# Second-layer modulation as rows, gate matrices stored by groups of experts, prompt rows without a wait

## The chip, the cores and the metric

The kernel runs on one core of a Trainium2 chip. The metric is the device time of one execution in microseconds, as the median of several runs. All data are in f32; the heavy matmuls of the expert layers split an f32 operand into two reduced-precision parts (`uh`, `ul` and so on) and multiply three of the four pairs.

## What is computed

One step of a two-layer network on two streams of tokens: a prompt of 128 tokens and a sample of 512, width 1024. Each layer has a mixer (retention with a gated convolution in layer 0, gated DeltaNet with a convolution module in layer 1) and a layer of retrieved experts. Both are modulated by a vector for each stream:

```python
def modulation(cvec, w, b):                      # cvec: one vector for the prompt, one for the sample
    m = jax.nn.silu(cvec) @ w + b                # w: 1024 x 6144 for each layer
    return jnp.split(m[:, None, :], 6, axis=-1)

def peer_ffn(h, wq, keys, u_tab, v_tab):         # 8 heads x 16 of 16384 experts for each token
    ...
    act = jax.nn.gelu(jnp.einsum('td,tkd->tk', xt, u_tab[et]))
    return jnp.einsum('tk,tkd->td', gt * act, v_tab[et])
```

Two vectors make the modulation of a layer: a product of 2 x 1024 with 1024 x 6144.

## The kernel before

The streams are called `sp` (prompt) and `ss` (sample), each cut into tiles of 128 tokens. The order of the program is: the mixer of layer 0 for both streams; `peer_dense(ss, 0)`, the expert layer of the sample, with the prompt's work of layer 1 (`odd_p`, called as `mid`) inside it; the sample's mixer of layer 1; `peer_dense(ss, 1)`; the final norm.

The experts are computed in two ways. Three of the four sample tiles go through all 128 groups of 128 experts densely. For the fourth sample tile and for the prompt each retrieved row of the tables `u` and `v` is fetched by an indirect DMA on GpSimd (`fetch`, L1226 on) into one of six row buffers, and VectorE multiplies it: 128 rows of `u` (L1256), then 128 of `v` (L1266, into `gacc`). These are called prompt rows and sample rows here.

`peer_dense` (L1386 on) has these stages for a layer:

1. Projection (`peer_prep`). From here on a generator, `acts`, runs behind the other work: for each group of experts it loads 512 KB of `u`, splits it on ScalarE and VectorE (L1336, L1337), multiplies it with the three tiles in 24 matmuls into `A`, applies the gelu on ScalarE (L1360) and stores the result to `wd` in memory. `tick` hands it out by the time of the matmuls of the foreground, at a rate for each stage.
2. Top keys (`peer_topk`, four tiles, mostly on VectorE). In layer 0 the modulation of layer 1 is made here: at each of the 24 steps of this stage three steps of the generator `modgen` are taken (L1210). A step loads 512 KB of modulation weights on SP into a ring of three buffers (`MW`, the phase's tag `w`).
3. Gates (`gate_matrix`). For each 16 tokens of the three tiles a matrix of 128 x 128 gates for each token is built on VectorE, TensorE and ScalarE and written to memory (`gd`) as one DMA of 1 MB, 24 for a layer. The pool of this stage lies where the top keys' space and the modulation's weights lay.
4. `mid`, in layer 0 only: the prompt's mixer of layer 1 and its top keys.
5. The dense loop: for each of 128 groups of experts, `v` (512 KB), the stored activations and the gates are loaded from memory, multiplied, split, and put through 18 matmuls into `dacc`. The gates of eight groups (`GQ`) are loaded at once, in three DMAs of 512 KB. In layer 1, 53 groups are fused: their activations are computed in this loop.

In the first four stages the order of GpSimd's instructions is that of the program, and a planner with a cost model orders those of the other engines. In the dense loop the order on GpSimd, VectorE and ScalarE is that of the program.

How many gathered rows go with each group of experts in the background is set by constants: `GP` for prompt rows in the top-key and gate stages of each layer, `STEPS` for sample rows there and in `mid`, `SP` and `SF` for sample rows in the dense loop. `self.mark` is the gelu of the newest group; while it is set, and `side_rate` is zero (as it is in the stages of top keys, gates and `mid`), each gather waits for it:

```python
f = self.nc.gpsimd.indirect_dma_start(...)
if self.mark and not self.side_rate:
    self.tc.add_manual_dep(f.ins, self.mark.ins.name, ...)
```

The modulation of layer 1 is made by TensorE with the weights as the stationary operand (L350 to L354): one of 48 column groups at a time, eight products of a 128 x 128 block of weights with two columns, `c_cols[:, k, :]`, the two vectors. The result is in columns, as the mixers use it.

Of the kernel before, what the change touches and what calls it, by code (L numbers as in the profile page):

```python
# [9 lines left out]
F32 = mybir.dt.float32  # L10
# [4 lines left out]
OP = mybir.AluOpType  # L15
PSUM = bass.MemoryType.PSUM

P = 128
D = 1024
KC = 8  # L20
# [5 lines left out]
TB = 16  # L26
GQ = 8
# [3 lines left out]
NB2 = 15  # L31
NT1 = 21
RP = 0.05
GP = (1.1, 2.0)
RQ = 0.055
SQ = (0.4, 0.46)
LE = 2
# [7 lines left out]
RG = 0.12  # L45
RH = 0.27
RM = 0.7
STEPS = ({"topk": 0.0, "gates": 0.0, "mid": 2.2}, {"topk": 0.3, "gates": 0.35})
UB = 2
VB = 3  # L50
WB = 3
# [32 lines left out]
class Kern:  # L84
# [254 lines left out]
    def modulation(self, l, part):  # L339

        nc, V = self.nc, self.nc.vector
        lo, hi = PARTS[part]
        m = self.cp.tile([P, hi - lo, 2], F32, name=f"mod{l}{part}")
        on_pe = range(lo, hi) if l == 1 else range(lo + 1, hi, 2) if part == 0 else ()
        if on_pe:
            b = self.bank("mod", (P, len(on_pe), 2))
        for n in range(lo, hi):
            w = self.mw("w")
            if n in on_pe:
                nc.sync.dma_start(w, self.A[f"ada_k{l}"][on_pe.index(n) + (lo if l else 0)])  # L350
                for k in range(KC):
                    nc.tensor.matmul(b[:, on_pe.index(n), :], w[:, k * P:(k + 1) * P], self.c_cols[:, k, :],
                                     start=(k == 0), stop=(k == KC - 1))
            else:  # L354
                nc.sync.dma_start(w, self.A["ada_c"][n])
                scr = self.mw("scr")
                for s in range(2):
                    V.scalar_tensor_tensor(scr if s == 0 else w, w, 1.0, self.c_rows[s], op0=OP.mult, op1=OP.mult,
                                           accum_out=m[:, n - lo, s:s + 1])
            yield  # L360
        if on_pe:
            V.tensor_copy(m[:, on_pe.start - lo::on_pe.step, :], b)
        V.scalar_tensor_tensor(m, m, 0.5, self.ada_b[:, l, lo:hi].unsqueeze(2).to_broadcast([P, hi - lo, 2]),
                               op0=OP.mult, op1=OP.add)
        if part in (0, 2):
            g = self.gains[:, 2 * l + part // 2, :]
            V.scalar_tensor_tensor(m[:, 8:16, :], m[:, 8:16, :], 1.0, g.unsqueeze(2).to_broadcast([P, KC, 2]),
                                   op0=OP.add, op1=OP.mult)
        self.mods[l, part] = m
# [856 lines left out]
    def fetch(self, table, idx):  # L1226
        t = self.rt("row")
        f = self.nc.gpsimd.indirect_dma_start(out=t, out_offset=None, in_=table,  # L1228
                                              in_offset=bass.IndirectOffsetOnAxis(ap=idx, axis=0))
        if self.mark and not self.side_rate:  # L1230

            self.tc.add_manual_dep(f.ins, self.mark.ins.name,
                                   mybir.DependencyInfo(mybir.DependencyClass.Sync, mybir.DependencyReason.DATA))
        return t
# [56 lines left out]
    def gate_matrix(self, st, tiles, gd):  # L1291

        nc = self.nc
        V, S, PE = nc.vector, nc.scalar, nc.tensor
        for n, it in enumerate(tiles):
            cols = self.gp.tile([P, 4, P], F32, tag="gcols", bufs=1, name=self.nm("gcols"))
            for j in range(2):
                ii = self.gp.tile([P, P], I32, tag="gi", name=self.nm("gi"))
                if j == 0:
                    V.tensor_scalar(ii, st.eid[it], 7, None, op0=OP.logical_shift_right)  # L1300
                else:
                    V.tensor_scalar(ii, st.eid[it], 127, None, op0=OP.bitwise_and)
                fi = self.gp.tile([P, P], F32, tag="gf", name=self.nm("gf"))
                V.tensor_copy(fi, ii)
                b = self.bank("gT", (P, P))
                self.transpose_to(b, fi)
                V.tensor_copy(cols[:, j, :], b)
            b = self.bank("gT", (P, P))
            self.transpose_to(b, st.gate[it])
            V.tensor_copy(cols[:, 2, :], b)  # L1310
            V.tensor_scalar(cols[:, 3, :], cols[:, 0, :], -1.0, None, op0=OP.mult)
            for tb in range(P // TB):
                out = self.gp.tile([P, P, TB], F32, tag="gst", bufs=3, name=self.nm("gst"))
                for q in range(TB // 4):
                    t = tb * TB + q * 4
                    o2 = self.gp.tile([P, 4, P], F32, tag="o2", bufs=4, name=self.nm("o2"))
                    V.tensor_tensor(o2, self.iota128.unsqueeze(1).to_broadcast([P, 4, P]),
                                    cols[:, 1, t:t + 4].unsqueeze(2).to_broadcast([P, 4, P]), op=OP.is_equal)
                    b = self.bank("G", (P, 4, P))
                    for j in range(4):  # L1320
                        t = tb * TB + q * 4 + j
                        o1 = self.gp.tile([P, P], F32, tag="o1", bufs=16, name=self.nm("o1"))
                        if j == 3:

                            S.activation(o1, self.iota128, AF.Square, bias=cols[:, 3, t:t + 1])
                            S.activation(o1, o1, AF.Relu, scale=-1.0, bias=cols[:, 2, t:t + 1])
                        else:
                            V.tensor_scalar(o1, self.iota128, cols[:, 0, t:t + 1], cols[:, 2, t:t + 1],
                                            op0=OP.is_equal, op1=OP.mult)
                        self.mm(b[:, j, :], o2[:, j, :], o1, start=True, stop=True)  # L1330
                    S.copy(out[:, :, q * 4:q * 4 + 4], b.rearrange("p t i -> p i t"))
                nc.sync.dma_start(gd[n * (P // TB) + tb], out)

    def split(self, hi, lo, src):

# [50 lines left out]
    def peer_dense(self, st, l, mid=None):  # L1386

        nc, A = self.nc, self.A
        V, S, PE = nc.vector, nc.scalar, nc.tensor
        tiles, gt = list(range(st.nt - 1)), st.nt - 1  # L1390
        N = len(tiles) * P
        NTB = N // TB
        gd = self.tc.dram_tile([NTB, P, P, TB], F32, name=self.nm("gd"))
        wd = self.tc.dram_tile([P, P, N], F32, name=self.nm("wd"))
        n = FUSED[l]
        LA = (LA0, LA1)[l]
        fused = {e for e in range(4, P) if e * n // P != (e + 1) * n // P}
        gg, got = {}, {}
# [4 lines left out]
        def load(e):  # L1403

            if e >= P:
                return
            vr = ld("vr", [P, D], bufs=LA + 1)
            nc.sync.dma_start(vr, A[f"v{l}"][e * P:(e + 1) * P, :])
            for n in range(0, NTB, 8):
                if e == 0 or e % GQ == 4 + n // 8 and e + GQ < P:  # L1410
                    g = e // GQ + (e > 0)
                    if n == 0:
                        gg[g] = ld("gt", [P, NTB, GQ, TB], bufs=2)
                    nc.sync.dma_start(gg[g][:, n:n + 8],
                                      gd[n:n + 8, :, g * GQ:(g + 1) * GQ, :].rearrange("b p i t -> p b i t"))
            if e in fused:
                w = self.u_load(l, e, up, UB)
            else:
                w = ld("w", [P, N], bufs=LA + 1)
                nc.sync.dma_start(w, wd[e])  # L1420
            got[e] = [vr, w, gg[e // GQ]]
# [6 lines left out]
        with self.banks(5), self.tc.tile_pool(name=self.nm("up"), bufs=2, reuse_waits="tile") as up:  # L1428
# [13 lines left out]
            self.rate, self.side_rate = RA, 0.0  # L1442
            self.steps_per_act, self.side_per_act = STEPS[l]["topk"], GP[l]
            with self.topk_space():
# [28 lines left out]
        with ExitStack() as c2:  # L1473
# [33 lines left out]
            for e in range(P):  # L1507
# [12 lines left out]
                for n in range(len(tiles)):  # L1520
                    ts = slice(n * P, (n + 1) * P)
                    for i, wh, wl, vh, vl in ends:
                        for lhs, rhs, fi, la in ((wh, vh, True, False), (wh, vl, False, False), (wl, vh, False, True)):
                            for half in range(2):
                                self.mm(accs[n][half], lhs[:, ts], rhs[:, half * 512:(half + 1) * 512],
                                        start=(i == 0 and fi), stop=(i == P - 1 and la))
# [5 lines left out]
            g = self.bcast_cols(self.mod(l, 3)[:, :, st.s:st.s + 1], "ga2", [gr[:, 0:512], gr[:, 512:1024]], self.bankA)  # L1532
# [149 lines left out]
def _chunks(w):  # L1682

    n = w.shape[1] // P
    return np.ascontiguousarray(w.reshape(KC, P, n, P).transpose(2, 1, 0, 3)).reshape(n, P, KC * P)


def _halves(w):

    return np.ascontiguousarray(w.reshape(4, 2, P, 512).transpose(0, 2, 1, 3)).reshape(4, P, 1024)  # L1690


def _cols(v):

    return np.ascontiguousarray(v.reshape(-1, P).T)


def device_inputs(inp):
    a = {k: np.asarray(v) for k, v in inp.items()}
    d = dict(_constants())  # L1700
    d["x_p"], d["x_s"] = a["x_prompt"][0], a["x_sample"][0]
    d["cT"] = np.ascontiguousarray(np.stack([_cols(a["c_ctx"]), _cols(a["c"][0])], axis=2))
    d["ada_k0"], d["ada_k1"] = _chunks(a["ada_w"][0])[1:16:2], _chunks(a["ada_w"][1])
    d["c_rows"] = np.stack([a["c_ctx"], a["c"][0]])
    d["ada_c"] = np.ascontiguousarray(a["ada_w"][0].T).reshape(48, P, D)
    d["ada_b"] = np.ascontiguousarray(np.stack([_cols(a["ada_b"][l]) for l in range(2)], axis=1))
# [12 lines left out]
    w = a["ev_w_in"][0]  # L1719
    t = _chunks(w)  # L1720
    q, bg, cg, hb = t[0:4], t[12:16], t[16:20], t[20:24]
# [3 lines left out]
    w = a["od_w_in"][0]  # L1725
# [40 lines left out]
```

## Time and profile before

| | us |
|---|---|
| median of three runs (lowest, highest) | 4222.24 (4215.71, 4222.56) |
| profiled execution, its own time | 4210.32 |
| its span, first to last instruction | 4208.6 |
| TensorE busy | 3844.7 (91%) |
| VectorE busy | 3396.4 (81%) |
| ScalarE busy | 1501.1 (36%) |
| GpSimd busy | 1455.3 (35%) |

The rows below come from one profiled execution; times are counted from the start of its span. "PE" is TensorE, "PEld" its weight loads, "DVE" VectorE, "ACT" ScalarE, "POOL" GpSimd and "SP" the engine that issues most DMAs. A clock of 1.00 is 2.4 GHz, 0.50 is 1.2 GHz. Most matmuls and many helpers go through one line (L162), so the tile's name says what an instruction belongs to: `A` is an expert's activation, `dacc` the dense accumulation, `mod` the modulation, `gacc` the gathered rows' sum. An f32 matmul appears as two instructions.

### The profile page before, as it was taken

How to read it: one execution, taken by the hardware profiler on the slowest of the kernel's cores; microseconds unless marked ns; L12 is line 12 of the kernel's file. 1: busy time of each engine (PE TensorE's matmuls, PEld its weight loads, DVE VectorE, ACT ScalarE, POOL GpSimd, SP SyncE). 2: the span in 40 equal slices, each digit the busy share in tenths (PEclk: the TensorE clock that was granted, in tenths of full speed). 3: DMA queues.
4: the chain of work that ended last, by engine and by line, in shares of the span. 5: the costliest groups of instructions: out<-in, count | busy, mean ns of one | idle time of the engine just before them, and what ended most of it. 6: DMA issues, size and time to landing. Idle time of an engine off the chain costs nothing. (4 is left out here: it accounts for less than half of the span.)

```text
span 4208.6 us, 57302 instructions
## 1 busy us (share of the span) xinstructions
PE 3844.7 (91%) x19934; PEld 3246.7 (77%) x19934; DVE 3396.4 (81%) x7163; ACT 1501.1 (36%) x2796; POOL 1455.3 (35%) x1080
## 2 busy tenths in 40 slices
PE   6788879999999998899998989789989989999997
PEld 4453559999998897688885458759989968888886
DVE  6568799993898975988887999669887877778888
ACT  2110133221565443333332254533335733333333
POOL 0106563111233342344434765033010024444443
PEclk9999589877999999999999999999999999999998
DMA  8539698657899988999997977158355789999996
GB/s 293 180 132 365 217 349 289 239 210 248 279 330 349 339 290 287 319 365 357 352 319 300 336 246 258 55 173 296 110 188 196 259 311 325 326 330 329 343 339 217
DMA packets 439634, 1162.04 MB, mean 276 GB/s; under 512 B 39728, under 2 KB 190640, under 8 KB 432944
## 3 DMA queue, kind: packets, MB, share of 16 engines
q1 hardware_dynamic: 284656, 595.23, 40.5%
q0 software_dynamic: 154688, 563.15, 37.7%
q8 instruction: 156, 2.56, 0.2%
q14 instruction: 134, 1.10, 0.1%
HBM read 1062.48 MB, written 95.75 MB: 275 GB/s over the span
## 5 line engine op out<-in xcount | busy, mean ns | idle before, releaser
L1228 POOL DMA_INDIRECT row<-v,eid x512 | 740.8, 1447 | 1331.3 <-DVE gacc L1266 607.2
L162 PE MATMUL A<-hHL,uh 128*128 128x384 f32 x4096 | 1101.7, 349 | 20.1 <-ACT uh L1336 19.2
L1228 POOL DMA_INDIRECT row<-u,eid x512 | 684.9, 1338 | 1153.3 <-ACT w L1360 483.3
L162 PEld LDWEIGHTS A<-hHL,uh 128*128 128x128 f32 x4096 | 768.9, 196 | 32.4 <-ACT uh L1336 23.6
L162 PE MATMUL A<-hHL,ul 128*128 128x384 f32 x2048 | 714.1, 350 | 44.3 <-DVE ul L1337 44.1
L1266 DVE SCALAR_TENSOR_TENSOR gacc<-row,gel,gacc 128x1024 f32<-128x1024 f32 x508 | 650.4, 1280 | 100.2 <-DMA row<-v,eid 95.6
L1256 DVE SCALAR_TENSOR_TENSOR row<-row,hn 128x1024 f32<-128x1024 f32 x512 | 614.2, 1218 | 114.1 <-DMA row<-u,eid 112.6
L162 PE MATMUL dacc<-vh,wh 128*128 128x512 f32 x1536 | 483.5, 396 | 51.3 <-ACT wh L1336 51.3
L162 PE MATMUL pt<-hT,w 128*128 128x128 f32 (+1 forms) x2176 | 456.5, 367 | 27.7 <-DMA w<-wq 15.6
L162 PE MATMUL dacc<-vl,wh 128*128 128x512 f32 x1536 | 477.6, 392 | 0.0
L1336 ACT CAST uh<-ur 128x1024 fp32r<-128x1024 f32 x256 | 268.3, 1048 | 563.8 <-PE A L162 441.8
L162 PEld LDWEIGHTS A<-hHL,ul 128*128 128x128 f32 x2048 | 400.5, 196 | 53.5 <-DVE ul L1337 52.1
L162 PEld LDWEIGHTS pt<-hT,w 128*128 128x128 f32 x2176 | 306.0, 197 | 171.4 <-issue 145.8
L162 PE MATMUL dacc<-vh,wl 128*128 128x512 f32 x1536 | 391.4, 389 | 0.0
L162 PEld LDWEIGHTS dacc<-vh,wh 128*128 128x128 f32 x1536 | 283.2, 189 | 124.7 <-ACT wh L1336 73.6
L1336 ACT CAST wh<-w 128x384 fp32r<-128x384 f32 (+1 forms) x235 | 137.5, 585 | 660.5 <-DVE w L1498 471.6
L1337 DVE TENSOR_TENSOR ul<-ur,uh 128x1024 fp32r<-128x1024 f32 x256 | 311.8, 1218 | 75.5 <-ACT uh L1336 75.0
L1337 DVE TENSOR_TENSOR vl<-vr,vh 128x1024 fp32r<-128x1024 f32 x256 | 312.8, 1222 | 65.6 <-ACT vh L1336 63.4
L162 PEld LDWEIGHTS dacc<-vl,wh 128*128 128x128 f32 x1536 | 290.9, 189 | 62.7
L162 PEld LDWEIGHTS dacc<-vh,wl 128*128 128x128 f32 x1536 | 288.6, 188 | 60.1
L1336 ACT CAST vh<-vr 128x1024 fp32r<-128x1024 f32 x256 | 267.7, 1046 | 57.3 <-PE dacc L162 48.7
L1337 DVE TENSOR_TENSOR wl<-w,wh 128x384 fp32r<-128x384 f32 (+1 forms) x235 | 152.2, 648 | 126.4 <-ACT wh L1336 126.3
(365 smaller groups left out, 5096.0 us busy)
## 6 DMA issues: line engine op xcount, KB each, us to landing
ur<-ut SPq DMA_DIRECT2D x256, 512.0 KB, 4.9
vr<-v SPq DMA_DIRECT2D x256, 512.0 KB, 6.8
gd<-gst SPq DMA_DIRECT2D x48, 1024.0 KB, 5.2
gt<-gd SPq DMA_DIRECT2D x96, 512.0 KB, 8.8
wd<-w SPq DMA_DIRECT2D x203, 192.0 KB, 3.4
w<-wd SPq DMA_DIRECT2D x203, 192.0 KB, 6.9
w<-ada_k SPq DMA_DIRECT2D x56, 512.0 KB, 6.0
w<-wq SPq DMA_DIRECT2D x48, 512.0 KB, 5.2
```

What stands on the lines that cost most here:

```text
L162: self.nc.tensor.matmul(out, lhsT, rhs, start=start, stop=stop)
L1228: f = self.nc.gpsimd.indirect_dma_start(out=t, out_offset=None, in_=table, in_offset=bass.IndirectOffsetOnAxis(ap=idx, axis=0))
L1256: V.scalar_tensor_tensor(u, u, 1.0, hn, op0=OP.mult, op1=OP.mult, accum_out=act[:, k:k + 1])
L1266: V.scalar_tensor_tensor(gacc, v, t[:, k:k + 1], gacc, op0=OP.mult, op1=OP.add)
L1336: self.nc.scalar.copy(hi, src)
L1337: self.nc.vector.tensor_tensor(lo, src, hi.bitcast(F32), op=OP.subtract)
```

## The change

The modulation of layer 1 turns its operands round. The two vectors are the stationary operand (128 x 2) and the weights move, 512 columns at a time: for each of twelve groups of 512 outputs, eight products, two for each weight load of 512 KB. The result is two rows of 512, which ScalarE copies from PSUM into a buffer of the weights' ring; four small transposes on TensorE bring it back into columns, and VectorE copies these. The modulation of layer 0 stays as it was. The number of generator steps (48) and of loads (48 of 512 KB) stays too.

The gate matrices are stored as `[group of 8, 128, blocks of tokens, 8, 16]` instead of `[block of tokens, 128, 128, 16]`: a write of 1 MB now goes to 16 places for each partition, 512 B each, and a load of 512 KB reads 4 KB in one piece for each partition, where it read eight pieces of 512 B.

Gathers wait for the newest expert's gelu if they belong to the sample (an empty `lane`) and no longer by the stage; prompt rows (`lane` "p") never wait for it. And three constants go up: 1.5 prompt rows for each group of experts in layer 0 (1.1 before), and 0.45 and 0.6 sample rows in the top-key and gate stages of layer 1 (0.3 and 0.35 before).

```diff
-GP = (1.1, 2.0)
+GP = (1.5, 2.0)
-STEPS = ({"topk": 0.0, "gates": 0.0, "mid": 2.2}, {"topk": 0.3, "gates": 0.35})
+STEPS = ({"topk": 0.0, "gates": 0.0, "mid": 2.2}, {"topk": 0.45, "gates": 0.6})
...
+            for o in range(lo // 4, hi // 4):
+                b = self.bank("mod")
+                for kp in range(KC // 2):
+                    w = self.mw("w")
+                    nc.sync.dma_start(w, self.A["ada_m1"][o, kp])
+                    for k in (2 * kp, 2 * kp + 1):
+                        nc.tensor.matmul(b[0:2, :], self.c_cols[:, k, :], w[:, (k % 2) * 512:(k % 2 + 1) * 512],
+                                         start=(k == 0), stop=(k == KC - 1))
+                    yield
+                t = self.mw("modr")[0:2, 0:512]
+                nc.scalar.copy(t, b[0:2, :])
+                b = self.bank("modT", (P, 4, 2))
+                for j in range(4):
+                    nc.tensor.transpose(b[:, j, :], t[:, j * P:(j + 1) * P], self.ident[0:2, 0:2])
+                V.tensor_copy(m[:, 4 * o - lo:4 * o - lo + 4, :], b)
...
-        if self.mark and not self.side_rate:
+        if self.mark and not self.lane:
...
-                nc.sync.dma_start(gd[n * (P // TB) + tb], out)
+                nc.sync.dma_start(gd[:, :, n * (P // TB) + tb].rearrange("g p q t -> p g q t"),
+                                  out.rearrange("p (g q) t -> p g q t", q=GQ))
...
-        gd = self.tc.dram_tile([NTB, P, P, TB], F32, name=self.nm("gd"))
+        gd = self.tc.dram_tile([P // GQ, P, NTB, GQ, TB], F32, name=self.nm("gd"))
...
-                    nc.sync.dma_start(gg[g][:, n:n + 8],
-                                      gd[n:n + 8, :, g * GQ:(g + 1) * GQ, :].rearrange("b p i t -> p b i t"))
+                    nc.sync.dma_start(gg[g][:, n:n + 8], gd[g, :, n:n + 8])
```

## Rows read from the trace of the kernel before

**Rows 1.** The page's first part: busy time of each engine, share, instructions.
```profile
PE 3844.7 (91%) x19934; PEld 3246.7 (77%) x19934; DVE 3396.4 (81%) x7163; ACT 1501.1 (36%) x2796; POOL 1455.3 (35%) x1080
```
**Rows 2.** Windows: stretch, length, busy PE, PEld, DVE, ACT, POOL; clock, DMA share, GB/s.
```profile
800.00:1060.00 260.00, 256.59 (x1438) 255.27 (x1437) 170.18 (x491) 51.48 (x69) 44.94 (x31) 0.78 0.66 233
1060.00:1340.00 280.00, 262.16 (x1739) 256.86 (x1738) 261.97 (x554) 172.89 (x376) 90.91 (x68) 0.99 0.89 318
```
**Rows 3.** The modulation's own busy time in that window; then timeline, start and length.
```profile
800.00:1060.00 260.00, 110.93 (x768) 112.31 (x768) 2.71 (x14) 0.00 (x0) 0.78 0.66 233
...
1042.92 7.05 PE L352 MATMUL mod<-c_cols,w 128*128 128x2 f32 x48
...
1050.31 0.22 DVE L1300 TENSOR_SCALAR gi<-eid 128x128 int32<-128x128 int32 x1
```
**Rows 4.** Timeline of the stretch: two modulation blocks that follow each other.
```profile
964.36 7.00 PE L352 MATMUL mod<-c_cols,w 128*128 128x2 f32 x48
...
981.25 6.84 PE L352 MATMUL mod<-c_cols,w 128*128 128x2 f32 x48
```
**Rows 5.** Windows of one microsecond around the first of these blocks.
```profile
966.00:967.00 1.00, 1.00 (x11) 1.00 (x10) 0.15 (x1) 0.00 (x0) 0.92 (x1) 1.00 1.00 397
967.00:968.00 1.00, 1.00 (x10) 1.00 (x11) 1.00 (x1) 0.00 (x0) 0.69 (x2) 0.95 1.02 376
...
970.00:971.00 1.00, 1.00 (x6) 1.00 (x6) 0.00 (x0) 0.00 (x0) 0.00 (x0) 0.50 1.11 283
...
976.00:977.00 1.00, 1.00 (x8) 1.00 (x7) 0.00 (x0) 0.00 (x0) 0.00 (x0) 1.00 0.47 193
```
**Rows 6.** Timeline: f32 matmuls, transposes; chain of waits: one expert's matmuls.
```profile
2439.78 5.74 PE L162 MATMUL pn<-w,hT 128*128 128x512 f32 x13
...
210.99 1.04 PE L416 MATMUL xT<-cst,xn 128*128 128x128 f32 x8
...
4153.44 4.16 PE A L162 x24
```
**Rows 7.** A window in the sample's retention, and the timeline at its end.
```profile
440.00:450.00 10.00, 10.00 (x33) 7.81 (x34) 8.31 (x15) 2.58 (x10) 7.66 (x5) 0.50 0.82 263
...
447.76 5.49 PE L162 MATMUL s<-qk,qk 64*128 64x512 f32 x6
```
**Rows 8.** Windows of line L1266 (v rows), VectorE; list of waits: total, times, longest.
```profile
800.00:1060.00 260.00, 37.48 (x30) 0.78 0.66 233
1060.00:1210.00 150.00, 34.55 (x27) 1.00 0.86 301
...
POOL row L1228 <- ACT w L1360: 753.8, 94, 139.7
```
**Rows 9.** DMA issues by line: count, KB each, median us to landing.
```profile
vr<-v SPq DMA_DIRECT2D x256, 512.0 KB, 6.8
gd<-gst SPq DMA_DIRECT2D x48, 1024.0 KB, 5.2
gt<-gd SPq DMA_DIRECT2D x96, 512.0 KB, 8.8
...
w<-ada_k SPq DMA_DIRECT2D x56, 512.0 KB, 6.0
```
**Rows 10.** Windows of the two dense loops, layer 0 and layer 1.
```profile
1690.00:2205.00 515.00, 499.77 (x2184) 410.32 (x2185) 443.35 (x606) 190.66 (x251) 210.60 (x118) 0.99 0.99 346
3420.00:4183.00 763.00, 739.52 (x3510) 636.22 (x3508) 614.58 (x773) 256.45 (x356) 335.51 (x229) 1.00 0.93 324
```
**Rows 11.** Windows, layer 1 before its loop: all engines, then L1256 (u rows, two records each).
```profile
3000.00:3400.00 400.00, 350.29 (x2189) 340.65 (x2189) 334.95 (x1006) 207.15 (x421) 32.80 (x21) 0.96 0.60 205
...
3000.00:3420.00 420.00, 25.47 (x42) 0.95 0.62 213
```
**Rows 12.** Timeline of the end: the dense tiles' last additions, and the gathered tile.
```profile
4186.95 1.87 DVE L1289 TENSOR_TENSOR x_s<-x_s,dacc 128x512 f32<-128x512 f32 x3
...
4194.01 1.29 DVE L1288 TENSOR_TENSOR gacc<-gacc,vr 128x512 f32<-128x512 f32 x2
```

More of the change, by code (lines that the diff above doesn't have):

```diff
@@ L343, in modulation @@
         m = self.cp.tile([P, hi - lo, 2], F32, name=f"mod{l}{part}")
[L344 to L360, printed above, removed]
@@ L361, in modulation @@
-        if on_pe:
-            V.tensor_copy(m[:, on_pe.start - lo::on_pe.step, :], b)
+        if l == 0:
+            on_pe = range(lo + 1, hi, 2) if part == 0 else ()
+            if on_pe:
+                b = self.bank("mod", (P, len(on_pe), 2))
+            for n in range(lo, hi):
+                w = self.mw("w")
+                if n in on_pe:
+                    nc.sync.dma_start(w, self.A["ada_k0"][on_pe.index(n)])
+                    for k in range(KC):
+                        nc.tensor.matmul(b[:, on_pe.index(n), :], w[:, k * P:(k + 1) * P], self.c_cols[:, k, :],
+                                         start=(k == 0), stop=(k == KC - 1))
+                else:
+                    nc.sync.dma_start(w, self.A["ada_c"][n])
+                    scr = self.mw("scr")
+                    for s in range(2):
+                        V.scalar_tensor_tensor(scr if s == 0 else w, w, 1.0, self.c_rows[s], op0=OP.mult, op1=OP.mult,
+                                               accum_out=m[:, n - lo, s:s + 1])
+                yield
+            if on_pe:
+                V.tensor_copy(m[:, on_pe.start - lo::on_pe.step, :], b)
+        else:
+            for o in range(lo // 4, hi // 4):
+                b = self.bank("mod")
+                for kp in range(KC // 2):
+                    w = self.mw("w")
+                    nc.sync.dma_start(w, self.A["ada_m1"][o, kp])
+                    for k in (2 * kp, 2 * kp + 1):
+                        nc.tensor.matmul(b[0:2, :], self.c_cols[:, k, :], w[:, (k % 2) * 512:(k % 2 + 1) * 512],
+                                         start=(k == 0), stop=(k == KC - 1))
+                    yield
+                t = self.mw("modr")[0:2, 0:512]
[4 more added lines that the diff above has]
+                V.tensor_copy(m[:, 4 * o - lo:4 * o - lo + 4, :], b)
@@ L1702, in device_inputs @@
     d["cT"] = np.ascontiguousarray(np.stack([_cols(a["c_ctx"]), _cols(a["c"][0])], axis=2))
-    d["ada_k0"], d["ada_k1"] = _chunks(a["ada_w"][0])[1:16:2], _chunks(a["ada_w"][1])
+    d["ada_k0"] = _chunks(a["ada_w"][0])[1:16:2]
+    d["ada_m1"] = np.stack([_halves(a["ada_w"][1][:, o:o + 512]) for o in range(0, 6 * D, 512)])
     d["c_rows"] = np.stack([a["c_ctx"], a["c"][0]])
```

## The prediction, made before the result was known

> **What bounds the kernel now.** I read the busy times first [rows 1]: TensorE is busy for 91% of the span and VectorE for 81%, so a saving must come from a stretch where TensorE has no gaps, and VectorE must have room for what is pushed together. Then the windows by stage [rows 2]. The stretch from 800 to 1060 us, in which the first expert layer picks its top keys and the second layer's modulation is made, stands out: TensorE is busy for 256.6 of 260 us, but its mean granted clock is 0.78, while the stretch behind it has 0.99. VectorE is busy for only 170 us there. The expert-weighting stage (gate matrix) cannot begin before the last modulation matmul, because its pool takes over the memory of the modulation's weights: the last block of 48 modulation matmuls starts at 1042.9 us and lasts some 7 us, and the first gate instruction starts at 1050.31 [rows 3]. So TensorE's time in this stretch is on the path.
>
> The timeline inside the stretch is periodic [rows 4]: a block of 48 modulation instructions (three weight tiles, 16 each) begins at 964.36 and the next at 981.25, a period of 16.9 us. The stretch has 768 such instructions [rows 3], 16 periods. The block takes 7.0 us, the two experts' matmuls behind it 9.9. In windows of one microsecond [rows 5] the clock is full at 966, begins to fall at the end of 967, is half at 970 (in the block) and full again at 976, well into the experts' matmuls. The modulation now loads 128x128 weights to stream two columns, and the chip takes the clock down to 1.2 GHz under it.
>
> **The modulation as rows.** Removed: 384 products of two columns, 768 instructions. Added: 96 products with two stationary columns and 512 moving ones, two instructions each as for any f32 matmul here, 192 in all, 12 for three weight tiles. Thirteen f32 matmuls of 512 columns take 5.74 us at full clock [rows 6]; less the 0.59 us of the last, that is 0.429 us from start to start. Twelve take 5.15 us. Two experts are 48 instructions; 24 take 4.16 us at full clock [rows 6], so 8.3 us. Per period there are three of the 48 small transposes (eight take 1.04 us [rows 6], less one's 0.27: 0.11 each) and a little wait, 0.4 us. The new period is 8.3 + 5.15 + 0.4 = 13.9 us instead of 16.9 if the clock stays full: 3.0 us x 16 = 48 us. Note where it comes from: at full clock the old block would need about as long as the new one (its instructions come twice as densely before 968 as after). The gain is the clock, 1.8 us in the block and 1.6 in the experts behind it, less the transposes.
>
> Added beside it: 12 ScalarE copies and 12 instead of 4 small VectorE copies; ScalarE is busy for 51 of 260 us [rows 2], so they are covered. The transposes wait for the copy, and the next expert's matmuls stand behind them on TensorE: nothing if the planner puts an expert in between, up to 12 x 1.5 us = 18 us if not (ScalarE's instructions there average 51.48 / 69 = 0.75 us [rows 2]; the copy and one ahead of it); I take the 6 us that stand in the period. The copied row takes one of the three weight buffers, so 60 allocations pass where 48 did; a weight load lands in 6.0 us [rows 9] and the experts behind a block last 8.3, so it still fits, with 2 us left. The loads stay 48 of 512 KB on SP.
>
> Does it reach the end? VectorE must do its 170 us in 212. Prompt rows freed from their wait add to that (below): 27 of them are now done after 1060 at 1.28 us [rows 8], 35 us; if all move ahead, 205 of 212 us are full. So I take 40 of the 48.
>
> **Prompt rows without the wait.** In the top-key and gate stages each prompt gather now waits for the newest expert's activation: 754 us of GpSimd waiting are put down to it [rows 8], and 30 v rows go through in 260 us although VectorE has room for more. After it they flow as buffers come free, and 1.5 instead of 1.1 go with each expert. The work is the same; 27 rows leave the gate stage of 1060 to 1340, where VectorE is busy for 262 of 280 us. Bound: -35 us if that stage is VectorE's alone, +10 us if rows stand ahead of the splits that TensorE waits for; TensorE is busy for 262 there too, so I take -5.
>
> **Gate matrices by groups.** Each of 48 writes of 1 MB goes from runs of 8 KB to runs of 512 B, each of 96 reads from 512 B to 4 KB. Price of short runs: the 512 KB gate read lands in 8.8 us, the 512 KB load of v issued just ahead of it in 6.8 [rows 9]. Of the 2.0 us 1.5 is its own transfer at 346 GB/s [rows 10], so 0.5 us per 512 KB is left, 1 us for a write: 24 us of queue in a 280 us stage whose DMA share is 0.89, to 0.97. Ends: 0 and, with the whole 2.0 us, 96 us of queue, which would fill that stage; I take the near one, 0 us on the path, SP and the three gate buffers absorbing it. The dense stages lose 24 us of queue each at a share of 0.99 and 0.93, but TensorE is busy there for 500 of 515 and 740 of 763 us [rows 10]: -4 us, ends 0 and -20. The Trainium skill (Perfetto Trace Analysis, DMA Optimizations) says transfers under 2 KB carry a significant overhead each; by that the writes would cost more than I allow. The reads of 512 B here show at most 0.5 us per 512 KB; no run yet shows such writes.
>
> **More sample rows early in layer 1.** 21 u rows (42 records) are now done before the dense loop [rows 11]; that loop steps 53 x 2.3 + 75 x 1.5 = 234 rows, so some are left over and end the kernel: VectorE adds the last dense tile by 4188.82 but starts scaling the gathered rows at 4194.01 [rows 12]. Rates of 0.45 and 0.6 for 0.3 and 0.35 bring some 10 rows forward: the leftover is gone, -5 us (0 to -8). They cost 10 x 1.3 = 13 us of VectorE in 3000 to 3400, where it is busy for 335 of 400 [rows 11]: 0 to 13, I take +3.
>
> **Sum.** -40 - 5 + 0 - 4 - 5 + 3 = -51 us. The profiled execution took 4210.3 us (span 4208.6), 11.9 below the median of the runs, 4222.2. From 4210.3 to 4159; on the median, 4171.
>
> **The rivals.** They hang on one question the trace cannot settle: whether two stationary columns keep the clock up. Against it: from 440 to 450 TensorE is busy without a gap, on a mix of 64-row and 128-row matmuls, and has half clock all along [rows 7]; a busy engine is not enough, part of the array in use may count. For it: those lack rows, while the new matmuls use all 128 rows and stream without gaps. The Trainium skill (TensorE: Matmul & The Clock Gate, Why this matters for your kernels) says to keep TensorE busy continuously to get full clock; by that my forecast holds, but [rows 7] disagree with it as it stands.
>
> Rival 1, the clock falls as now: nine matmuls in the 3.9 us before it falls, three at 0.86, 6.4 us, plus 0.5 and the 9.9 us of experts: 16.8, no gain. The rest gives -11: 4211. On the median between 4203 and 4228.
>
> Rival 2, slower: the clock stays low through every block, as it does at 440. Twelve at 0.86 us are 10.3, plus 0.6 and 9.9: 20.8, +3.9 x 16 = +62, less 11: 4273, 4235 to 4290. It decides if a block starts at 0.50.
>
> Rival 3, VectorE takes over: the clock holds, but the freed rows and the top keys fill VectorE, and the gate stage waits for it. The gain is halved to 20: 4191.
>
> Rival 4, more gain: the gate stage is VectorE's and gives back 35 us: about 4140.
>
> **How the numbers follow.** Forecast 0.52 (4150 to 4190), rival 1 0.23, rival 2 0.12, rival 3 0.08, rival 4 0.05. About 0.2% (8 us) can be told from no change here. Faster: forecast, rivals 3 and 4 and a third of rival 1, 0.72. Same: most of the rest of rival 1, 0.14. Slower: rival 2 and a little of rival 1, 0.14. The range goes from rival 4's end to the end of rival 1: 4135 to 4230; rival 2 and a little at the other end are left out.
>
> **What would show it.** Right: a granted clock near 1.0 from 800 on, modulation matmuls of 512 columns 0.43 us apart, the first gate instruction near 1010 and the layer's dense loop some 45 us earlier. Wrong: windows of 0.5 in the blocks (rivals 1, 2); a full clock but VectorE without gaps up to the gate stage (rival 3). For the rows: POOL's waits for the expert's activation well under 754 us, prompt rows done by about 1060. For the layout: gate reads nearer to 6.8 us, and gate writes not far above their 5.2 us [rows 9]. For the tail: gathered rows scaled right after the last dense tile.

## The result, and the profile after

| | before | after |
|---|---|---|
| median of the runs, us (lowest, highest) | 4218.98 (4213.36, 4222.56) | 4158.94 (4148.63, 4168.12) |
| ratio after to before, 95% interval | | 0.9858 (0.9831 to 0.9885) |
| profiled execution, its own time | 4210.32 | 4148.63 |
| its span | 4208.6 | 4146.9 |

The change takes off 60 us (49 to 71). The prediction said 4171, 4135 to 4230, faster. In the profiled executions the span is 61.7 us shorter, and the page's first part says where: TensorE is busy for 3808.5 us instead of 3844.7 [rows 1], 36.2 less, so the other 25.5 us are gaps on TensorE that closed.

```profile
PE 3808.5 (92%) x19406; PEld 3124.2 (75%) x19406; DVE 3393.6 (82%) x7171; ACT 1510.3 (36%) x2810; POOL 1457.4 (35%) x1080
```

The windows of after (stretch, length, busy PE, PEld, DVE, ACT, POOL with their instructions, clock, DMA share, GB/s) answer to [rows 2], [rows 10] and the tail:

```profile
800.00:1060.00 260.00, 255.58 (x1110) 167.74 (x1108) 208.43 (x532) 70.23 (x95) 77.05 (x47) 0.99 0.81 294
1060.00:1340.00 280.00, 267.36 (x1852) 262.83 (x1852) 255.12 (x647) 175.32 (x388) 67.61 (x50) 0.99 0.89 297
...
1652.00:2156.00 504.00, 497.26 (x2172) 408.15 (x2173) 433.17 (x553) 187.07 (x247) 210.45 (x118) 1.00 0.95 347
3330.30:4146.00 815.70, 759.71 (x3592) 653.49 (x3592) 643.01 (x818) 273.19 (x389) 333.29 (x226) 0.97 0.87 315
```

In the stretch of the modulation the granted clock went from 0.78 to 0.99. TensorE is as busy as before (255.6 and 256.6 us), and what changed is what it did: 192 of its 1110 instructions are the modulation and 48 the small transposes, which leaves 870, 36 experts of 24, where before 768 of 1438 left 670, 28 experts. The stretch did eight experts more, 8 x 4.16 = 33 us of TensorE at full clock [rows 6].

The modulation's own busy time in that window, and the timeline of TensorE around the place of [rows 4]:

```profile
800.00:1060.00 260.00, 88.99 (x192) 12.79 (x192) 0.99 0.81 294
...
960.89 5.31 PE L372 MATMUL mod<-w,c_cols 128*2 128x512 f32 x12
969.28 1.88 PE L372 MATMUL mod<-w,c_cols 128*2 128x512 f32 x4
975.28 0.40 PE L379 MATMUL modT<-cst,modr 2*128 2x2 f32 x4
```

The block of twelve takes 5.31 us where the one of 48 took 7.0 [rows 4]; the stretch's total is 88.99 us instead of 110.93 [rows 3].

The last matmul of the modulation did not come earlier. The first row below is its group (duration in ns: lowest, median, highest; then first and last start), the second the first gate instruction, which stands behind it at 1064.83 and stood at 1050.31 [rows 3].

```profile
L372 PE MATMUL mod<-w,c_cols x192: 591/592/593, 815.0 to 1059.6; 128*2 128x512 f32 x192
...
1064.83 0.22 DVE L1318 TENSOR_SCALAR gi<-eid 128x128 int32<-128x128 int32 x1
```

The gate stage is what got shorter. From its first copy of a gate matrix to its last it took 259.1 us before (1071.2 to 1330.3) and 193.9 after (1079.7 to 1273.6). Prompt rows are out of it; the windows of their `v` rows (the line that was L1266 [rows 8]):

```profile
800.00:1060.00 260.00, 67.13 (x53) 0.99 0.81 294
1060.00:1210.00 150.00, 0.00 (x0) 0.99 0.78 247
```

All 53 lie in the first stretch, where 30 and 27 lay in the two. The dense loop of layer 0 begins at 1652.6 instead of 1698.8, 46 us earlier, and takes 503.4 us in both. The last gate copy of layer 1 is at 3330.3 instead of 3385.3, 55 us earlier, and the span ends 62 us earlier.

### The profile page after: what moved, and what is told of

It reads as the page before. It is cut to its first block, busy times and chain, and to the rows that moved or that the text cites. A ratio compares the mean times of both kernels' runs of the same rounds, so it can differ in the third digit from the quotient of the medians.

```text
span 4146.9 us, 56434 instructions
## 1 busy us (share of the span) xinstructions
PE 3808.5 (92%) x19406; PEld 3124.2 (75%) x19406; DVE 3393.6 (82%) x7171; ACT 1510.3 (36%) x2810; POOL 1457.4 (35%) x1080
## 5 line engine op out<-in xcount | busy, mean ns | idle before, releaser
L1246 POOL DMA_INDIRECT row<-v,eid x512 | 751.1, 1467 | 1084.4 <-DVE gacc L1284 629.8
L162 PE MATMUL A<-hHL,uh 128*128 128x384 f32 x4096 | 1085.0, 344 | 14.6 <-ACT uh L1355 11.3
L162 PEld LDWEIGHTS A<-hHL,uh 128*128 128x128 f32 x4096 | 748.6, 191 | 46.6 <-issue 20.3
L162 PE MATMUL A<-hHL,ul 128*128 128x384 f32 x2048 | 705.3, 345 | 44.7 <-DVE ul L1356 44.6
L162 PEld LDWEIGHTS A<-hHL,ul 128*128 128x128 f32 x2048 | 391.4, 191 | 67.5 <-DVE ul L1356 51.0
```

What stands on the lines that cost most here:

```text
L162: self.nc.tensor.matmul(out, lhsT, rhs, start=start, stop=stop)
```

## The experiments

Two questions: which part of the change gives how much, and why. The ratios are to the kernel before, run on the same chip between the others; the microseconds are the ratio's distance from 1 times 4217.

| | modulation | prompt rows | layout | sample rates | ratio (95%) | us |
|---|---|---|---|---|---|---|
| e1 | new | old | old | old | 0.9902 (0.9878 to 0.9927) | -41 |
| e2 | old | new | old | old | 0.9962 (0.9945 to 0.9980) | -16 |
| e5 | old | old | new | old | 1.0045 (1.0028 to 1.0063) | +19 |
| e6 | old | old | old | new | 0.9963 (0.9946 to 0.9979) | -16 |
| e10 | old | new | new | old | 0.9966 (0.9951 to 0.9981) | -14 |
| e3 | old | new | new | new | 0.9913 (0.9890 to 0.9936) | -37 |
| e9 | new | old | new | new | 0.9933 (0.9911 to 0.9954) | -28 |
| e7 | new | new | old | new | 0.9865 (0.9847 to 0.9882) | -57 |
| e8 | new | new | new | old | 0.9864 (0.9845 to 0.9884) | -57 |
| after | new | new | new | new | 0.9858 (0.9831 to 0.9885) | -60 |

**The modulation alone, put into the kernel before.**

```diff
-                    nc.tensor.matmul(b[:, on_pe.index(n), :], w[:, k * P:(k + 1) * P], self.c_cols[:, k, :],
+                        nc.tensor.matmul(b[0:2, :], self.c_cols[:, k, :], w[:, (k % 2) * 512:(k % 2 + 1) * 512],
```

> The kernel before with the modulation as rows alone. Theory C (clock): the gain is TensorE's clock under the modulation; the experts that it does more of by 1060 us are missing from the gate stage. Then this alone gives most of the gain, 35 to 48 us of the 60, and the granted clock of 800 to 1060 is near 1.0. Theory V (VectorE): the gate stage became shorter because the prompt rows left it. Then this gives 10 us at most, and the gate stage stays near 285 us.

The weights are stored in another order for this, still 4 KB in one piece for each partition and load. Measured: 4178.44 (4174.98 to 4188.68), 41 us less than before (31 to 51). The window from 800 to 1060 has a granted clock of 0.99 and VectorE is busy for 191.6 us of it. TensorE is busy for 3817.1 us in the whole, 27.6 less than before. So the modulation gives most of the 60 us under the old rule for the rows too. Its profiled execution (4180.92) is 29.4 us under before's: the gate stage takes 234.5 us instead of 259.1, the dense loop of layer 0 begins 17 us earlier, and another 12 us are gained later, between the first addition of a dense tile in layer 0 and the last gate copy of layer 1 (1142.1 us instead of 1154.0), where nothing of the new modulation runs. That last part is not explained.

**The prompt rows alone.**

```diff
-GP = (1.1, 2.0)
+GP = (1.5, 2.0)
-        if self.mark and not self.side_rate:
+        if self.mark and not self.lane:
```

> The kernel before with the prompt rows' part alone (no wait for the experts, 1.5 instead of 1.1 with each in layer 0). Theory C: between -10 and +5 us, as TensorE's work in 800 to 1060 stays at a clock of 0.78. Theory V: -25 to -40 us, with the gate stage near 240 us.

Measured: 4206.77 (4188.73 to 4211.94), 16 us less (8 to 23). The gate stage ends 32 us earlier, at 1298.7, but the dense loop of layer 0 begins only 9 us earlier, at 1689.4: the experts that the shorter gate stage no longer covers are done in `mid`. From the end of the gate stage to the dense loop TensorE has 2282 instructions (2173 before); the 109 more are 4.5 experts, 19 us at 4.16 [rows 6]. This profiled execution is the slowest of e2's ten (4211.94) and ends 1.6 us after before's, with 10 us more in layer 1; so the trace shows what happens in the two stages, and not where the 16 us of the medians come out.

**The old modulation in the changed kernel.**

```diff
-                    for k in (2 * kp, 2 * kp + 1):
-                        nc.tensor.matmul(b[0:2, :], self.c_cols[:, k, :], w[:, (k % 2) * 512:(k % 2 + 1) * 512],
+                    nc.tensor.matmul(b[:, on_pe.index(n), :], w[:, k * P:(k + 1) * P], self.c_cols[:, k, :],
```

> The changed kernel with the old modulation back. Theory C: 40 to 55 us slower than the changed kernel (4200 to 4215 us), clock back to about 0.78 in 800 to 1060. Theory V: at most 10 us slower.

Measured: 4182.73 (4177.66 to 4188.70), 24 us slower than the changed kernel (8 to 38 by the two ratios), for the 41 of e1 (31 to 51); these overlap. TensorE is busy for 3835.4 us, 26.9 more than in the changed kernel. So on TensorE's own time the new modulation is worth 27 us in both places; what reaches the end is 24 to 41 by the two medians. And the three other parts together give 37 us here, where the prediction had 11. That opened the question that the next runs are about.

**Half of the rows of the array.** The products of the modulation run over 64 of the 128 rows, so half of each sum is left out.

```diff
-nc.tensor.matmul(b[0:2, :], self.c_cols[:, k, :], w[:, (k % 2) * 512:(k % 2 + 1) * 512],
+nc.tensor.matmul(b[0:2, :], self.c_cols[0:64, k, :], w[0:64, (k % 2) * 512:(k % 2 + 1) * 512],
```

> The changed kernel with the modulation's products over 64 of the 128 rows, so that half of each sum is left out; as many instructions of the same length. If the chip counts the rows of the array that are in use, as the 64-row matmuls near 440 us suggest, the clock falls to 0.5 in the modulation blocks and the kernel loses 30 to 60 us. If it counts matmuls in flight only, the clock stays at 1.0 and the time within 10 us of the changed kernel's.

Measured, one execution: 4187.50 us, granted clock 0.96 from 800 to 1060. This windows view of three microseconds each is of e4:

```profile
959.00:962.00 3.00, 3.00 (x13) 1.35 (x11) 3.00 (x4) 0.00 (x0) 0.00 (x0) 1.00 0.64 242
962.00:965.00 3.00, 1.79 (x9) 1.31 (x9) 3.00 (x4) 1.42 (x2) 0.00 (x0) 1.00 0.10 35
965.00:968.00 3.00, 3.00 (x7) 0.53 (x7) 3.00 (x4) 0.03 (x1) 0.00 (x0) 0.74 0.91 276
968.00:971.00 3.00, 3.00 (x10) 3.00 (x11) 3.00 (x4) 0.55 (x1) 0.00 (x0) 0.50 0.91 289
971.00:974.00 3.00, 3.00 (x13) 3.00 (x12) 0.26 (x1) 0.00 (x0) 0.00 (x0) 0.62 0.41 165
974.00:977.00 3.00, 3.00 (x20) 2.74 (x19) 2.20 (x3) 1.44 (x2) 0.00 (x0) 1.00 0.37 96
```

The blocks between 902 and 962 keep the full clock with half of the rows. Where it falls next, that is behind a gap: TensorE is busy for 1.79 of the 3 us from 962 (it waits 1.21 us for a split), and then the clock is 0.74 and 0.50 with no gap left. The changed kernel does the same behind the one long gap of its stretch from 800 to 1060, 2.04 us at 837 to 839:

```profile
836.00:839.00 3.00, 1.09 (x8) 0.62 (x6) 3.00 (x5) 2.71 (x3) 1.54 (x2) 1.00 1.03 420
839.00:842.00 3.00, 2.87 (x12) 2.87 (x13) 3.00 (x7) 0.00 (x1) 2.27 (x2) 0.72 1.02 406
842.00:845.00 3.00, 3.00 (x14) 2.81 (x12) 3.00 (x5) 0.14 (x1) 0.49 (x1) 0.71 1.04 420
845.00:848.00 3.00, 3.00 (x8) 0.59 (x8) 3.00 (x5) 1.40 (x2) 2.35 (x1) 1.00 1.03 388
```

Not every gap is followed by a fall. In e4 one of 2.85 us, longer than either, ends at 845.2, and the clock is full on both sides of it:

```profile
841.00:845.00 4.00, 1.36 (x9) 0.78 (x7) 4.00 (x6) 2.71 (x3) 2.37 (x2) 1.00 1.03 412
845.00:849.00 4.00, 3.79 (x22) 3.79 (x23) 4.00 (x8) 0.00 (x0) 0.94 (x1) 1.00 1.03 414
```

So half of the rows did not take the clock down, in blocks of 1.9 to 3.6 us with experts on the whole array between them; a longer run of such matmuls was not tried. The old blocks have another shape, two moving columns for each 128x128 of weights, and no gap in the record [rows 5]. What in them took the clock down was not taken apart; shown is that turning the operands round ended it. The time of this one execution, some 28 us above the changed kernel's median, fits neither expectation (30 to 60, or within 10) and is not settled: it has 24 us of gaps on TensorE from 800 to the end of its gate stage, the changed kernel 13.

**The layout alone, and the sample rates alone.**

```diff
-        gd = self.tc.dram_tile([NTB, P, P, TB], F32, name=self.nm("gd"))
+        gd = self.tc.dram_tile([P // GQ, P, NTB, GQ, TB], F32, name=self.nm("gd"))
```

> The kernel before with the gate layout alone. The old modulation with freed prompt rows, the new layout and the new sample rates came out 37 us below before, the freed prompt rows alone 13: some 24 us belong to the layout, to the sample rates, or to neither alone. Theory L (layout): reads in one piece for each partition end stalls of the dense loops and the gate stage: 15 to 20 us less, near 4202, the dense loops shorter. Theory S (sample rows) and theory N (where the planner puts the experts once rows move, no part by itself): within 5 us of before, 4215 to 4224, both dense loops within 3 us of 504 and 799 us.

```diff
-STEPS = ({"topk": 0.0, "gates": 0.0, "mid": 2.2}, {"topk": 0.3, "gates": 0.35})
+STEPS = ({"topk": 0.0, "gates": 0.0, "mid": 2.2}, {"topk": 0.45, "gates": 0.6})
```

> The kernel before with 0.45 and 0.6 sample rows in the top-key and gate stages of layer 1 alone. Theory S: the gathered rows no longer end the kernel and fill gaps of VectorE in layer 1: 15 to 20 us less, near 4202. Theory L and theory N: 2 us less (the tail -5, the extra VectorE time +3, as predicted), between 4207 and 4225; the last gathered row is added before the last dense tile in any case.

Measured: the layout alone is slower, 4238.17 (4222.56 to 4242.74), 19 us (12 to 27), which no theory had. The rates alone give 4201.65 (4191.93 to 4212.51), 16 us less (9 to 23), as theory S had it.

**Each of these two taken back in the changed kernel** (the same diffs, read backwards).

> The changed kernel with the gate matrices stored by blocks of tokens as before. Theory L: 15 to 20 us slower than the changed kernel, near 4176. Theory S and N: within 6 us of it, 4155 to 4165; its gate writes are issued in 320 ns again instead of 370.

> The changed kernel with the old rates of sample rows in layer 1 (0.3 and 0.35). Theory S: 15 to 20 us slower than the changed kernel, near 4176, with gathered rows scaled some 5 us after the last dense tile again. Theory L and N: 2 us slower (0 to 8), 4159 to 4167.

Measured: 4159.74 (4157.49 to 4162.84) and 4160.68 (4155.33 to 4164.81). Neither can be told from the changed kernel, so theory L is out, and theory S with it as an account of the changed kernel. For the layout there are two numbers, +19 alone (12 to 27) and -3 here (-17 to 11 by the two ratios), whose intervals do not overlap, if only just. A new theory was needed: the parts meet in the gate stage.

**The theory of the meeting parts.** Two more kernels complete the square of prompt rows and layout. The first is the changed kernel with the two lines of e2's diff taken back, the second is before with e2's and the layout's diffs.

> The changed kernel with the old rule for the prompt rows (each gather waits for the newest expert's activation in these stages) and 1.1 of them with each group of experts. The layout alone made the kernel before 22 us slower, and taking it out of the changed kernel made no difference. Theory I (the parts meet: gate writes in short pieces cost time only while the gathers of prompt rows share the DMA queues of the gate stage): here both come together again, so this is slower than the changed kernel by the 13 us of the rows and the 22 us of the layout, near 4194 (4185 to 4200), with a gate stage at a DMA share of 0.9 or more and late loads of u. Theory A (each part has its own price, the 22 us are an accident of the order): 13 us slower, 4168 to 4177.

> The kernel before with the freed prompt rows (and 1.5 of them) and the gate layout, the other parts as before. Theory I: the rows have left the gate stage, so its writes have room: as the rows alone, 4200 to 4212. Theory A: the rows' 13 us off and the layout's 22 on, near 4226 (4220 to 4234).

Measured: 4186.81 (4181.21 to 4193.78), where theory I had 4185 to 4200 and theory A 4168 to 4177; and 4198.62 (4188.95 to 4212.63), where theory I had 4200 to 4212 and theory A 4220 to 4234. Both are theory I's, the second 1.4 us below its range. The prompt rows are worth 16 us with the old layout, and with the new one 33 (e5 to e10) and 32 (e9 to after). The layout costs 19 us while prompt rows are in the gate stage and, once they are out, +2 (e2 to e10) and -3 (e7 to after).

The profile shows how. Windows of the gate stage, first gate copy to last, one kernel each: before; the layout alone; rows and layout; old rows in the changed kernel; the old layout in it. After's own has the values 193.90 us, DMA share 0.90.

```profile
1071.20:1330.30 259.10, 243.20 (x1630) 238.89 (x1630) 245.53 (x520) 160.56 (x356) 84.70 (x62) 0.99 0.88 316
```
```profile
1078.80:1357.30 278.50, 251.41 (x1648) 247.33 (x1647) 246.89 (x520) 160.12 (x357) 81.12 (x63) 0.96 0.91 297
```
```profile
1066.00:1294.10 228.10, 220.51 (x1513) 217.10 (x1511) 191.19 (x454) 153.20 (x345) 38.24 (x29) 0.99 0.84 269
```
```profile
1081.20:1326.00 244.80, 217.89 (x1457) 212.79 (x1457) 227.56 (x504) 150.36 (x342) 79.90 (x57) 0.95 0.92 300
```
```profile
1087.70:1280.50 192.80, 184.56 (x1304) 182.00 (x1303) 184.03 (x453) 140.38 (x327) 38.32 (x31) 0.98 0.79 290
```

With the rows in the stage (GpSimd busy for some 80 us) the layout takes the DMA share from 0.88 to 0.91 while the rate falls from 316 to 297 GB/s: the queues work longer for the same bytes, and the stage gets longer. With the rows out (38 us) there is room: from 0.79 to 0.90 in the changed kernel, 0.90 x 193.9 - 0.79 x 192.8 = 22 us of queue for 24 writes (the other pairs that differ in the layout give 18 to 25), and the stage is as long as it was. The mean share does not tell after (0.90) from e5 (0.91). The first half of the stage does, where almost no rows are left in after; first e5, then after:

```profile
1078.80:1218.00 139.20, 135.89 (x919) 135.03 (x919) 125.55 (x250) 85.79 (x190) 36.28 (x27) 1.00 0.91 290
1079.70:1176.70 97.00, 97.00 (x723) 97.00 (x722) 91.46 (x241) 79.26 (x192) 1.33 (x2) 1.00 0.78 232
```

What the busy queues delay is read from the waits of that stage (waiter, awaited, us, times, longest): the loads of `u`, then the splits, then TensorE. Before, then e5, then after:

```profile
ACT uh L1336 <- DMA ur<-ut: 25.7, 9, 4.4
...
PEld A L162 <- ACT uh L1336: 14.5, 9, 3.9
```
```profile
ACT uh L1337 <- DMA ur<-ut: 49.6, 14, 6.0
...
PEld A L162 <- ACT uh L1337: 25.7, 10, 7.8
```
```profile
ACT uh L1355 <- DMA ur<-ut: 4.1, 3, 1.7
...
PEld A L162 <- ACT uh L1355: 0.9, 1, 0.9
```

ScalarE waits for late `u` 25.7 us before, 49.6 with the layout alone, 4.1 after. TensorE's weight loads wait 14.5, 25.7 and 0.9 us for the split behind it. The same wait in the stage in e1 and e9 (rows in, old and new layout; e9's sample rates act in layer 1 only), then in e2, e10 and e7 (rows out: old, new, old):

```profile
ACT uh L1354 <- DMA ur<-ut: 4.5, 2, 2.6
ACT uh L1355 <- DMA ur<-ut: 28.4, 7, 6.5
...
ACT uh L1336 <- DMA ur<-ut: 0.5, 1, 0.5
ACT uh L1337 <- DMA ur<-ut: 0.9, 2, 0.6
ACT uh L1354 <- DMA ur<-ut: 3.3, 3, 1.4
```

With the rows in, the layout adds 24 us of late `u` beside either modulation (25.7 to 49.6, 4.5 to 28.4); with the rows out it adds less than 1 (0.5 to 0.9, 3.3 to 4.1). This is what theory I says, and e9 had the share (0.92) and the late loads that it named. The rows alone do not make `u` late: e1 has them in the stage and waits 4.5 us. Not all of e5's distance is the stage's. Its profiled execution, the slowest of its six, is 32 us over before's: 8 are lost ahead of the stage, 19 in it and 5 in layer 1 ahead of its gates' end.

**How far this goes.** Two kernels on either side of the new constants:

```diff
-GP = (1.5, 2.0)
+GP = (1.35, 2.0)
```

> The changed kernel with 1.35 instead of 1.5 prompt rows for each group of experts, the smallest disturbance of the order that we could find: it measures what a mere reordering is worth. Theory I: the rows still end ahead of the gate stage, so nothing: 4152 to 4168. If prompt rows reach into the gate stage again, 5 to 15 us slower.

```diff
-GP = (1.5, 2.0)
-STEPS = ({"topk": 0.0, "gates": 0.0, "mid": 2.2}, {"topk": 0.45, "gates": 0.6})
+GP = (2.0, 2.0)
+STEPS = ({"topk": 0.0, "gates": 0.0, "mid": 2.2}, {"topk": 0.6, "gates": 0.9})
```

> The changed kernel with still more gathered rows early: 2.0 prompt rows for each group of experts, 0.6 and 0.9 sample rows in layer 1. Theory I: the prompt rows already end ahead of the gate stage, so nothing is left to win there: 4150 to 4170. A theory in which VectorE has room left in layer 1 gives up to 10 us less, 4145 to 4155.

Measured: 4156.64 (4142.23 to 4162.16), ratio to before 0.9865 (0.9839 to 0.9891), the same as the changed kernel; and 4169.59 (4164.69 to 4176.39), 0.9894 (0.9868 to 0.9921), some 11 to 15 us slower than the changed kernel by the medians and the ratios, though the intervals overlap. A little fewer rows change nothing, since they still end ahead of the gate stage; many more do not help. In e12 TensorE is busy for 250.6 us from 800 to 1060, five less than in the changed kernel, at a clock of 0.97: gaps opened there again. No kernel tried is better than the changed one by what can be measured.

## Why the prediction was right, point by point

**What bounds the kernel.** Right. The clock of the stretch from 800 to 1060 was the largest thing to win, and e1 alone has 41 of the 60 us.

**The modulation as rows.** The cause was right, and rivals 1 and 2 are out: the clock does not fall in the blocks. The size was not quite: the forecast was 3.0 us for each of 16 periods, 48, of which 40 reach the end. The stretch gained 33 us of experts, TensorE's busy time 27 (e1, and e3 against after), the runs 41 and 24. Of the terms, the block of twelve was put at 5.15 us and took 5.31 where it stands whole; over the stretch it is 88.99 / 16 = 5.56, because the planner cuts most blocks into fours (1.88 us each), and the experts cost (255.6 - 89.0 - 4.8) / 36 = 4.5 us, not the 4.16 of the fastest row. The 4.8 is 12 times the transposes' 0.40; that and the copy were put at 0.4 us a period, which held: ScalarE's copy takes 576 ns and one wait of 0.4 us is put down to it.

The place was wrong. The gate stage was to begin near 1010, and it began at 1065, later than before. The planner did not pull the modulation forward; it put eight more experts into the same stretch, and the saving arrived where these experts were missing, as a shorter gate stage. The dense loop of layer 0 then did begin 46 us earlier, for the 45 forecast.

The Trainium skill (TensorE: Matmul & The Clock Gate, Why this matters for your kernels) asks for a TensorE that is kept busy. The new blocks agree (clock 1.00 in 5.31 us without a gap); the old blocks do not, busy for 1.00 of 1.00 us at a clock of 0.50 [rows 5]. The doubt drawn from [rows 7], that rows in use may count, was answered by e4 for blocks of up to 3.6 us: 64 of 128 rows kept the full clock. What holds it at 0.50 from 440 to 450 stays open; TensorE is busy for only 31 of the 50 us from 400 on, and the two falls shown above follow gaps too.

**Prompt rows.** The step that was mis-sized. Forecast -5, bounds -35 to +10; measured -16 alone and some -32 with the new layout. The lower bound's reason (VectorE's time leaves the gate stage) was there: VectorE is busy for 191 us of it in e10, for 247 in e5. What the step did not see is the DMA side: the gathers of these rows left the stage too, and with them the late loads of `u` (25.7 us before, 0.5 in e2; 49.6 in e5, 0.9 in e10). The argument "TensorE is busy there too, so -5" took TensorE's gaps there, 18 us of that window [rows 2], for small. With the new layout it is these gaps that close: 27.1 us in the stage of e5 and 7.6 in e10's (278.5 - 251.4 and 228.1 - 220.5), 26.9 in e9's and 8.2 in after's, 19 of the 33 and 32 us. The stage's clock rises as well, from 0.96 to 0.99 and from 0.95 to 0.98; what that is worth was not measured by itself. With the old layout the clock there is 0.99 with the rows and without, 6 of 16 us of gaps close (e2), and where the rest of the -16 comes from stays open.

**Gate matrices by groups.** The price in queue was right and the cover was not named. Put at 1 us of queue for a write, measured 22 / 24 = 0.9 (0.7 to 1.1 over the pairs); put at 0.5 us for a read, measured (1.00 - 0.95) x 504 / 48 = 0.5 us, from the DMA share of layer 0's loop, 0.95 above and 1.00 in before's window of it:

```profile
1698.00:2202.00 504.00, 496.77 (x2171) 407.86 (x2172) 433.58 (x552) 187.61 (x246) 210.60 (x118) 1.00 1.00 348
```

The reading that the read's price came from does not hold, though. It took the 2.0 us by which a gate read lands after the load of `v` [rows 9] for the transfer and 0.5 us of short pieces. With reads in one piece the distance is as large; this is e11, the changed kernel with 1.35 rows:

```profile
vr<-v SPq DMA_DIRECT2D x256, 512.0 KB, 5.9
gd<-gst SPq DMA_DIRECT2D x48, 1024.0 KB, 6.1
gt<-gd SPq DMA_DIRECT2D x96, 512.0 KB, 8.0
```

That is 2.1 us (2.3 in e10, 1.7 in e9), and both loads land 0.8 to 0.9 us sooner than before.

The Trainium skill (Perfetto Trace Analysis, DMA Optimizations) warns of an overhead for each transfer under 2 KB. The trace agrees by the 0.9 us of queue for a write; the 19 us of e5 hold the shorter writes and the longer reads together. "0 on the path, SP and the buffers absorbing it" held only because the prompt rows had left the stage; had the two edits been costed one after the other at a share of 0.88, the 24 us would have had no room, as e5 shows. The gain in the dense loops, put at 4 us, did not come: 503.4 us in both kernels in layer 0, TensorE being busy for 497 of 504 in either, and in layer 1, from the last gate copy to the last dense addition, 803.5 before and 803.0 in e5. It matters for nothing that was measured here, and e7 says that the layout can go or stay.

**Sample rows.** Nine more `u` rows (152 instead of 143 in the window from the first dense loop's end to the last gate copy of layer 1) are done early, for the ten forecast, and the tail came as forecast: the last dense tile and the gathered one are now added side by side.

```profile
4127.48 0.68 DVE L1306 TENSOR_TENSOR gacc<-gacc,vr 128x512 f32<-128x512 f32 x1
4128.07 2.47 DVE L1307 TENSOR_TENSOR x_s<-x_s,dacc 128x512 f32<-128x512 f32 x4
4130.47 0.68 DVE L1307 TENSOR_TENSOR x_s<-x_s,gacc 128x512 f32<-128x512 f32 x1
```

From the last of these dense additions to the end of the span it is 16.4 us; before, 4208.6 - 4188.8 = 19.8 [rows 12]. That is 3.4 of the 5 us. In e8, without these rates, the gathered tile is again scaled 5 us behind the last dense addition, as it was before. The net was put at -2. Alone the rates gave -16 (e6) and -22 (e10 to e3), in the changed kernel -2 (e8), the last two within some 12 to 14 us either way. That they are worth more beside the old modulation is likely by this and not shown, and why is open: by the single profiles the stretch from the first addition of a dense tile in layer 0 to the last gate copy of layer 1 is 1154 to 1164 us in the four kernels that have neither the new modulation nor the new rates, and 1139 to 1154 in the ten that have either, but nothing in the modulation touches that stretch, and no run was made for it.

**The sum.** It came within 12 us in part by luck, because errors of both signs cancelled: the modulation some 8 too much by the mean of its two values, the prompt rows and the rates too little. Rival 3 (VectorE takes over) did not happen, though VectorE is full until about 1000, as feared: by then TensorE had experts enough to go on. Rival 4's mechanism, a gate stage given back, did happen and was hidden in the forecast's total, since `mid` took part of it back (e2's trace: 32 us won at the stage's end, 9 left at the dense loop).

**The signs to look for.** The clock, the 46 us and the prompt rows' end were right (the last of them is added at 971, forecast about 1060). Two signs were badly chosen. GpSimd's wait for the expert's activation was to be "well under 754 us" and is 702:

```profile
POOL row L1246 <- ACT w L1379: 702.0, 61, 226.1
```

One of its 61 waits is 226 us long: once the prompt rows are done, the first gather of the sample stands there from 949 to 1175, into the gate stage; whether that costs anything was not tried. The 0.43 us between products was right inside a block (twelve in 5.31). The landing times of gate reads and writes are not in the trace of after; in e11 the writes land in 6.1 us for 5.2, as the sign asked, and the reads in 8.0 for 8.8, nearer to 6.8 but not near it.

## What to carry to other kernels

A product with a vector or two is worth trying with the vectors stationary and the matrix moving, above all in the middle of other matmuls: here the old blocks' slow clock (0.50) was paid by the experts behind them too, and it showed as busy time. Cost the parts of a change in the stage where they meet, and look at the DMA share there as at an engine: shorter pieces were free where the share without them was 0.79 and cost 19 us where it was 0.88. And where a planner fills the gaps, a saving does not come out where it is made; count the work done in a stretch (experts here) beside its length.

## What the hardware showed that was not expected

Products over 64 of the 128 rows kept the full clock (1.00 from 902 to 962 in e4), while gaps of 1.21 and 2.04 us were followed by several microseconds at 0.50 to 0.74, and one of 2.85 us in e4 by the full clock. Twenty-four writes of 1 MB in pieces of 512 B took 22 us more of the DMA queues than in pieces of 8 KB (18 to 25 over the pairs), and SP needs 370 ns instead of 320 to issue one.
